# A full-height second product for the attention scores of a hybrid encoder kernel

## The chip, the core and the metric

The kernel runs on one NeuronCore of a Trainium2 chip (trn2). The metric is the device time of one execution in microseconds (us); lower is better. The core has a matrix engine (TensorE, written PE in the profile, with its weight loads as PEld), a vector engine (VectorE, DVE), a scalar engine (ScalarE, ACT) and a general engine (GpSimd, POOL). Each works through its own queue of instructions in order, and they wait for one another by semaphores. SyncE (SP) issues most transfers. Matrix products go to PSUM, which the kernel uses as 8 banks of 128x512 numbers.

## The reference

The model is a two-layer encoder on 512 positions of 1024 channels. Layer 0 has a differential softmax attention (4 heads, two maps per head, 64 channels per map) beside a recurrent branch; layer 1 has a Fourier mixer; each layer ends in a gated feed-forward net. The change touches the attention scores alone:

```python
s = jnp.einsum('bqhmd,bkhmd->bhmqk', qi, k) * scale      # 4 heads h, 2 maps m, d = 64
p = jax.nn.softmax(s - slopes * dist, axis=-1)
a = p[:, :, 0] - lam * p[:, :, 1]
o = jnp.einsum('bhqk,bkhd->bqhd', a, v)
o = rmsnorm(o, subln_g) * (1.0 - lam_init)
```

## The kernel before

Products run in a 32-bit format of the matrix engine that takes 12 significant bits of each number. A 32-bit number is therefore split into `hi` (rounded) and `lo` (the rest), and a product is made as hi·hi + hi·lo + lo·hi, three matmuls (`mm3`, lines 109 to 111). ACT makes `hi` by a copy, DVE makes `lo` by a subtraction (line 106 in `split`; for some weights POOL does it). Weights come in units of 1 MiB, as two halves `raw`, through three buffers, and are split into `whi` and `wlo`.

`proj_qk` (line 514) makes the queries and keys of two heads, channel by position: a PSUM tile `pqk` of 128 rows holds both maps of a head, 64 rows each (`halves`). For queries it builds, per map, a 128-row tile that stacks hi and lo of the map's 64 channels (lines 532 and 533): for map 0 it is [hi; lo], for map 1 [lo; hi]. For keys it builds per map [hi; hi] (two ACT copies, lines 539 and 540), and one tile `klo` for both maps with the key's rests (line 541, one DVE subtraction per map).

`scores(h, t)` makes the scores of head h and 128 queries t. Per map there are two products into one bank `psc`. The first (line 558) runs over all 128 rows: [hi; lo] against [hi; hi] gives hi·hi + lo·hi. The second (line 559) runs over the map's 64 rows alone: hi of the query against `klo`. Then DVE adds the position bias and finds the row maximum (line 561), negates it (line 563), ACT takes the exponential with its sum (through `act`, line 93), and DVE forms `p` from both maps (lines 566 to 568).

The loop over `steps` runs 16 steps (h, t). Step i issues `scores` of step i, a piece of other matrix work (`proj_qk(2)` in steps 0 to 7, `proj_yg` after that), two recurrent scans (lines 502 and 505, steps 0 to 3), and the later stages of earlier steps: `turn` of step i-2 transposes p into `paT` (line 580) and splits it into `aT`; `av` (tile `poT`) multiplies pairs of steps with the values; `norm_o` (lines 597 to 610, with the root on POOL at line 608) and `turn_o` (line 618) follow per head. After the loop the output projection starts (`proj_tok`, tile `pj`), with what is left of the last heads between its first products (`drain`).

Each engine's queue order is fixed when the kernel is built, by a scheduler that sees the program above and estimates times. A changed instruction can therefore move others on the same or other engines.

Of the kernel before, what the change touches and what calls it, by code (L numbers as in the profile page):

```python
# [16 lines left out]
P = 128  # L17
# [18 lines left out]
def encoder_kernel(  # L36
# [29 lines left out]
    def pair(name, dtype=F32):  # L66
        """two [128, 512] halves of a tile"""
        t_ = tile1k(name, dtype)
        return t_[:, 0:S], t_[:, S:2 * S]
# [7 lines left out]
    def f(ap):  # L77
        return ap.bitcast(F32)

    def order_after(ins, others):  # L80
        """ins stays behind others of its engine"""
        for b in others:
            tc.add_manual_dep(
                ins.ins, b.ins.name,
                mybir.DependencyInfo(mybir.DependencyClass.NoSync, mybir.DependencyReason.DATA),
                reason="order",
            )

    # Activations that need a table set run set by set, in program order.
# [10 lines left out]
    def split(hi, lo, src, hi_eng=A, lo_eng=V):  # L100
        """src = hi + lo exactly, both of 12 significant bits."""
        if hi_eng is A:
            A.copy(hi, src)  # L103
        else:
            hi_eng.tensor_copy(hi, src)
        lo_eng.tensor_tensor(out=lo, in0=src, in1=f(hi), op=ALU.subtract)  # L106
# [105 lines left out]
    def inv_rms(ssa, ssb, n):  # L212
        """((ssa + ssb) / n + eps) ** -0.5 of two [P, 1] sums, of which ssa comes first."""
        m0, m = sm("m"), sm("m")
        V.tensor_scalar(out=m0, in0=ssa, scalar1=n * EPS, scalar2=None, op0=ALU.add)
        V.tensor_scalar(out=m, in0=ssb, scalar1=m0, scalar2=1.0 / n, op0=ALU.add, op1=ALU.mult)  # L216
        return inv_sqrt(m)
# [18 lines left out]
    def pre_norm(t, g):  # L236
        """x tile t, normalised, as two halves"""
        xs_ = pair("xn")
        r = pre_stats(t, xs_)
        for h in range(2):  # L240
            sl = slice(h * S, (h + 1) * S)
            V.scalar_tensor_tensor(out=xs_[h], in0=xt[t][:, sl], scalar=r, in1=g[:, sl], op0=ALU.mult, op1=ALU.mult)
        xn[t] = xs_

    def turn_x(t):
        """the halves of pre_norm into hn as [channel, token], split"""
        for h, xh in enumerate(xn.pop(t)):
            pt = bank("pT")
            for k in range(4):
                T.transpose(pt[:, k * P:(k + 1) * P], xh[:, k * P:(k + 1) * P], ident)  # L250
            dst = slice(t * P, (t + 1) * P)
            pv = pt.rearrange("p (k c) -> p k c", c=P)
            split(hn["hi"][:, h * 4:h * 4 + 4, dst], hn["lo"][:, h * 4:h * 4 + 4, dst], pv)

    def post_norm(t, ps, g):
        """x tile t += rmsnorm(ps) * g"""
        ys = pair("y")
        ss = [sm("ss"), sm("ss")]
        for h in range(2):
            A.activation(ys[h], ps[h], AF.Square, accum_out=ss[h])  # L260
        r = inv_rms(ss[0], ss[1], D)
        for h in range(2):
            sl = slice(h * S, (h + 1) * S)
            y = ys[h]
            V.scalar_tensor_tensor(out=y, in0=ps[h], scalar=r, in1=g[:, sl], op0=ALU.mult, op1=ALU.mult)
            V.tensor_tensor(out=xt[t][:, sl], in0=xt[t][:, sl], in1=y, op=ALU.add)

    def proj_tok(ks, lhs, chunk, tail, finish, late=None, hook=None, spare=False):
        """[tok, D] = sum over the row tiles ks; the last `tail` of them token tile by
        token tile to the end, the others in chunks. With `spare`, two banks stay free  # L270
        and the last row tile is not needed until the first token tile ends."""
# [41 lines left out]
    def col_tiles(unit_list, consume, halves):  # L313
        """[col, tok] products of column tiles: unit_list holds (unit, column offset)."""
# [50 lines left out]
    # per-channel vectors: rows of 128, turned into columns by one transpose  # L365
# [56 lines left out]
    # lambda of the differential attention, on every partition  # L422
# [8 lines left out]
    # -(e1 - e2 + lam_init)  # L431
# [5 lines left out]
    # C * log_sigmoid(lam) = -C * (max(-lam, 0) + log1p(exp(-|lam|)))  # L437
# [24 lines left out]
    def make_gates(c):  # L462
        for d in range(2):
            g2 = pair("gate")
            for n, b_ in enumerate((ba, bi)):
                ps = bank("pg")
                o = (d * 4 + c) * P
                mm3(ps, [w[:, o:o + P] for w in ulru[n]], xcs[c], True, True)
                act(g2[n], ps, AF.Sigmoid, "sigmoid", bias=b_[:, d * 4 + c:d * 4 + c + 1])
            # i * xc  # L470
            last_ix[0] = G.tensor_tensor(out=g2[1], in0=g2[1], in1=xc[c], op=ALU.mult)
            gates[d, c] = g2

    # decays: a = exp(cl r) = 1 + q, q = expm1(cl r); sqrt(1 - a^2) = sqrt(-q (2 + q))
# [39 lines left out]
    def proj_qk(h0):  # L514
        """q and k of heads h0 and h0 + 1, in eight parts"""
        qh = {}
        for z in range(2):
            u = next_unit(1)
            for h in (h0, h0 + 1):
# [9 lines left out]
                if z == 0:  # L529
                    # [hi; lo] and [lo; hi]  # L530
# [4 lines left out]
                else:  # L535
                    # [hi; hi] twice, and lo
                    lo = tile1k("klo", F32R)[:, 0:S]
                    for m, sl in enumerate(halves):
                        A.copy(a[m][sl, :], ps[sl, :])
                        A.copy(a[m][halves[1 - m], :], ps[sl, :])  # L540
                        V.tensor_tensor(out=lo[sl, :], in0=ps[sl, :], in1=f(a[m][sl, :]), op=ALU.subtract)
# [6 lines left out]
    def scores(h, t):  # L548
        """p0 - lam (s0 / s1) p1 of unnormalised p; the norm that follows takes care of s0"""
# [5 lines left out]
        for m in range(2):  # L555
            sl = halves[m]
            ps = bank("psc")
            T.matmul(ps, lhsT=q_[m][:, t * P:(t + 1) * P], rhs=k_[m], start=True, stop=False)  # L558
            T.matmul(ps, lhsT=q_[m][sl, t * P:(t + 1) * P], rhs=klo[sl, :], start=False, stop=True)  # L559
# [13 lines left out]
    def turn(h, t):  # L573
        """[query, key] tile into [key, query], split"""
# [19 lines left out]
    def norm_o(h):  # L594
# [7 lines left out]
        # mean + eps s0^2  # L602
# [23 lines left out]
    def proj_yg():  # L626
        """gate columns, in eight parts"""
# [42 lines left out]
    def finish_step(i):  # L670
        """later stages of steps before i"""
# [27 lines left out]
    # what is left goes between the first products of the output projection  # L699
# [19 lines left out]
    def ffn(l, after, tail, hook=None):  # L719
# [11 lines left out]
        for u in range(NF // 2):  # L731
            # the first pair's products cover the norm's end: splits for later ones come after it
# [62 lines left out]
    # [p, (kt, cos|sin, c')]  # L795
# [10 lines left out]
    # over the positions: the last token tile after the others  # L806
# [17 lines left out]
    # over the channels of a group: E (even in k) and O (odd in k), F = E - O  # L824
# [16 lines left out]
    def mirror(c):  # L841
        """y[512 - k] = E + O, then y[k] = E - O in place of E"""
# [38 lines left out]
def _parts(a):  # L881
    """float64 -> [2, ...] float32: a value of 12 significant bits, and 12 bits of the rest."""
# [49 lines left out]
```

## Time and profile before

| | |
|---|---|
| time, median of 3 runs | 1058.29 us (1057.21 to 1058.57) |
| span of the profiled execution, first to last instruction | 1056.6 us |
| first products of the scores, line 558 | 32, median 494 ns each |
| second products of the scores, line 559 | 32, median 497 ns each |
| key rests, line 541 | 8 on DVE, median 690 ns each |
| the score products run from | 96.7 us to 186.5 us of the span |

The page gives the span of the profiled execution and not its whole time; the median of the runs is 1.7 us above the span, and that difference is taken as what lies around it. Rows of the timeline give the start, the duration, the engine, the source line, the operation with output<-inputs, its size, and in brackets the idle time of the engine just before it with what ended it. Durations of matmuls overlap, so the distance from one start to the next tells what a matmul costs, and the duration does not.

### The profile page before, as it was taken

How to read it: one execution, taken by the hardware profiler on the slowest of the kernel's cores; microseconds unless marked ns; L12 is line 12 of the kernel's file. 1: busy time of each engine (PE TensorE's matmuls, PEld its weight loads, DVE VectorE, ACT ScalarE, POOL GpSimd, SP SyncE). 2: the span in 40 equal slices, each digit the busy share in tenths (PEclk: the TensorE clock that was granted, in tenths of full speed). 3: DMA queues.
4: the chain of work that ended last, by engine and by line, in shares of the span. 5: the costliest groups of instructions: out<-in, count | busy, mean ns of one | idle time of the engine just before them, and what ended most of it. 6: DMA issues, size and time to landing. Idle time of an engine off the chain costs nothing.

```text
span 1056.6 us, 12277 instructions
## 1 busy us (share of the span) xinstructions
PE 1032.2 (98%) x4913; PEld 857.7 (81%) x4913; DVE 480.4 (45%) x760; ACT 391.1 (37%) x644; POOL 100.3 (9%) x94
## 2 busy tenths in 40 slices
PE   5999999999999999999999999999999999999997
PEld 4897677779888888888888888898888888888885
DVE  5969976754532332223233556645322223234304
ACT  5386676733522221122232455334221122223201
POOL 1057523211000000000100110100000000000000
PEclk9998999999999999999999999999999999999999
DMA  6531212311752333222533024027343223224002
GB/s 222 161 107 70 95 46 95 119 41 41 205 153 80 113 108 98 80 81 89 168 111 110 1 65 155 1 80 219 92 127 101 79 80 107 93 80 138 3 1 80
DMA packets 73123, 102.92 MB, mean 97 GB/s; under 512 B 3893, under 2 KB 61290, under 8 KB 73066
## 3 DMA queue, kind: packets, MB, share of 16 engines
q1 hardware_dynamic: 70442, 94.02, 28.7%
q0 software_dynamic: 2624, 8.13, 2.4%
q8 instruction: 38, 0.62, 0.2%
q14 instruction: 19, 0.16, 0.0%
HBM read 100.04 MB, written 2.10 MB: 97 GB/s over the span
## 4 chain that ended last, share of the span: by engine, by line
PE 94%; DVE 3%; ACT 1%; DMA 1%; issue 1%; POOL 0%; SPq 0%; DVEq 0%; POOLq 0%; ACTq 0%
PE pc L110 15%; PE pc L109 15%; PE pc L111 15%; PE pj L111 10%; PE pj L109 10%; PE pj L110 10%; PE pqk L109 1%; PE psc L559 1%; PE pqk L110 1%; PE pqk L111 1%; PE psc L558 1%; DMA raw<-in_w_in_dram 1%; PE pT L250 1%; PE pyg L109 1%; PE pv L111 1%; PE put L109 1%
## 5 line engine op out<-in xcount | busy, mean ns | idle before, releaser
L106 DVE TENSOR_TENSOR wlo<-raw,whi 128x1024 fp32r<-128x1024 f32 x158 | 190.9, 1232 | 272.2 <-ACT whi L103 221.1
L110 PE MATMUL pc<-hnlo,whi 128*128 128x512 f32 (+1 forms) x768 | 285.1, 372 | 0.0
L109 PE MATMUL pc<-hnhi,whi 128*128 128x512 f32 (+1 forms) x768 | 284.6, 372 | 0.5 <-ACT hnhi L103 0.5
L111 PE MATMUL pc<-hnhi,wlo 128*128 128x512 f32 (+1 forms) x768 | 284.9, 371 | 0.0
L103 ACT CAST whi<-raw 128x1024 fp32r<-128x1024 f32 x164 | 167.4, 1049 | 125.2 <-PE pj L110 31.0
L109 PEld LDWEIGHTS pc<-hnhi,whi 128*128 128x128 f32 x768 | 144.2, 188 | 26.1 <-ACT hnhi L103 1.0
L111 PEld LDWEIGHTS pc<-hnhi,wlo 128*128 128x128 f32 x768 | 144.7, 188 | 25.1
L110 PEld LDWEIGHTS pc<-hnlo,whi 128*128 128x128 f32 x768 | 144.7, 188 | 25.0 <-DVE hnlo L106 0.4
L109 PE MATMUL pj<-whi,gs 128*128 128x512 f32 x352 | 136.9, 389 | 0.0
L110 PE MATMUL pj<-wlo,gs 128*128 128x512 f32 x352 | 136.9, 389 | 0.0
L111 PE MATMUL pj<-whi,gs 128*128 128x512 f32 x352 | 136.9, 389 | 0.0
L93 ACT ACTIVATE gated<-pc 128x512 f32<-128x512 f32 x44 | 26.2, 597 | 268.6 <-PE pc L111 268.6
L729 DVE TENSOR_TENSOR gated<-gated,pc 128x512 f32<-128x512 f32 x44 | 30.2, 686 | 111.4 <-PE pc L111 111.4
L111 PEld LDWEIGHTS pj<-whi,gs 128*128 128x128 f32 x352 | 66.1, 188 | 13.8
L110 PEld LDWEIGHTS pj<-wlo,gs 128*128 128x128 f32 x352 | 66.1, 188 | 13.8
L109 PEld LDWEIGHTS pj<-whi,gs 128*128 128x128 f32 x352 | 66.1, 188 | 13.6
L209 POOL TENSOR_TENSOR r<-m,mhalf 128x1 f32<-128x1 f32 x32 | 17.5, 547 | 552.2 <-DVE m L216 552.2
L260 ACT ACTIVATE y<-pj 128x512 f32<-128x512 f32 x32 | 19.1, 597 | 82.3 <-PE pj L111 82.3
L103 ACT CAST gs<-gated 128x512 fp32r<-128x512 f32 x44 | 25.3, 618 | 52.2 <-PE pj L110 32.2
L106 DVE TENSOR_TENSOR gs<-gated,gs 128x512 fp32r<-128x512 f32 x44 | 28.4, 685 | 31.3 <-ACT gs L103 31.3
L106 POOL TENSOR_TENSOR wlo<-raw,whi 128x1024 fp32r<-128x1024 f32 x12 | 29.7, 2484 | 47.9 <-ACT whi L103 46.8
L93 ACT ACTIVATE p<-p,mx 128x512 f32<-128x512 f32 x32 | 23.1, 723 | 17.6 <-DVE mx L563 17.5
(190 smaller groups left out, 1282.5 us busy)
## 6 DMA issues: line engine op xcount, KB each, us to landing
raw<-in_w_ffn_gate_dram SPq DMA_DIRECT2D x44, 512.0 KB, 4.1
raw<-in_w_ffn_up_dram SPq DMA_DIRECT2D x44, 512.0 KB, 5.1
raw<-in_w_ffn_down_dram SPq DMA_DIRECT2D x44, 512.0 KB, 3.8
raw<-in_w_in_dram SPq DMA_DIRECT2D x20, 512.0 KB, 3.7
raw<-in_w_mix_out_dram SPq DMA_DIRECT2D x8, 512.0 KB, 3.3
raw<-in_w_fourier_out_dram SPq DMA_DIRECT2D x8, 512.0 KB, 4.3
pos<-in_dft_pos_dram POOLq DMA_DIRECT2D x8, 256.0 KB, 5.7
out_dram<-x SPq DMA_DIRECT2D x8, 256.0 KB, 2.1
```

Of the source, the lines that this page charges most:

```text
L93: ins = A.activation(out_, in_, func, **kw)
L103: A.copy(hi, src)
L106: lo_eng.tensor_tensor(out=lo, in0=src, in1=f(hi), op=ALU.subtract)
L109: T.matmul(ps, lhsT=l[0], rhs=r[0], start=start, stop=False)
L110: T.matmul(ps, lhsT=l[0], rhs=r[1], start=False, stop=False)
L111: T.matmul(ps, lhsT=l[1], rhs=r[0], start=False, stop=stop)
L209: G.tensor_tensor(out=r, in0=m, in1=mhalf[:, 0:1], op=ALU.pow)
L250: T.transpose(pt[:, k * P:(k + 1) * P], xh[:, k * P:(k + 1) * P], ident)
L260: A.activation(ys[h], ps[h], AF.Square, accum_out=ss[h])
L558: T.matmul(ps, lhsT=q_[m][:, t * P:(t + 1) * P], rhs=k_[m], start=True, stop=False)
L559: T.matmul(ps, lhsT=q_[m][sl, t * P:(t + 1) * P], rhs=klo[sl, :], start=False, stop=True)
L729: V.tensor_tensor(out=gated[fc], in0=gated[fc], in1=ps, op=ALU.mult)
```

## The change

The key rests are now built for each map as a 128-row tile [lo; lo] in place of 64 rows, so that the second product takes the whole stacked query: [hi; lo] against [lo; lo]. It adds the lo·lo part, which was left out before, and the number of matmuls stays. DVE makes each rest twice, once per half of the rows: 16 subtractions of 64x512 where there were 8. The tile pool serves the same number of tiles of the same size. (Comments were taken out as well; from the second added line on, lines up to 556 are numbered one higher.)

```diff
                 else:
-                    lo = tile1k("klo", F32R)[:, 0:S]
+                    lo = pair("klo", F32R)
                     for m, sl in enumerate(halves):
                         A.copy(a[m][sl, :], ps[sl, :])
                         A.copy(a[m][halves[1 - m], :], ps[sl, :])
-                        V.tensor_tensor(out=lo[sl, :], in0=ps[sl, :], in1=f(a[m][sl, :]), op=ALU.subtract)
+                        for to in halves:
+                            V.tensor_tensor(out=lo[m][to, :], in0=ps[sl, :], in1=f(a[m][sl, :]), op=ALU.subtract)
                     qks[h] = (qh[h], a, lo)
...
         for m in range(2):
-            sl = halves[m]
             ps = bank("psc")
             T.matmul(ps, lhsT=q_[m][:, t * P:(t + 1) * P], rhs=k_[m], start=True, stop=False)
-            T.matmul(ps, lhsT=q_[m][sl, t * P:(t + 1) * P], rhs=klo[sl, :], start=False, stop=True)
+            T.matmul(ps, lhsT=q_[m][:, t * P:(t + 1) * P], rhs=klo[m], start=False, stop=True)
```

The scheduler moves instructions of DVE, ACT, POOL and, in a few places, PE between the first scores and the output projection; the queue of SP is as it was. Three places follow.

On DVE, ahead of the first scores (`klo` is the key rest, `gate` the recurrent scans, `psc` the scores of step 0), before:

```order
L541 TENSOR_TENSOR klo_941<-pqk_915,qk_940 64x512
L505 SCALAR_TENSOR_TENSOR gate_563<-gate_563 128x512
L502 SCALAR_TENSOR_TENSOR gate_607<-gate_607 128x512
L541 TENSOR_TENSOR klo_941<-pqk_915,qk_940 64x512
L505 SCALAR_TENSOR_TENSOR gate_619<-gate_619 128x512
L502 SCALAR_TENSOR_TENSOR gate_695<-gate_695 128x512
L505 SCALAR_TENSOR_TENSOR gate_707<-gate_707 128x512
L502 SCALAR_TENSOR_TENSOR gate_719<-gate_719 128x512
L541 TENSOR_TENSOR klo_974<-pqk_948,qk_973 64x512
L561 ISA p_997,mx_1002<-psc_999,bias_839 128x512
```

and the same place with the change:

```order
L542 TENSOR_TENSOR klo_941<-pqk_915,qk_940 64x512 x2
L505 SCALAR_TENSOR_TENSOR gate_563<-gate_563 128x512
L502 SCALAR_TENSOR_TENSOR gate_607<-gate_607 128x512
L542 TENSOR_TENSOR klo_941<-pqk_915,qk_940 64x512 x2
L505 SCALAR_TENSOR_TENSOR gate_619<-gate_619 128x512
L502 SCALAR_TENSOR_TENSOR gate_695<-gate_695 128x512
L542 TENSOR_TENSOR klo_976<-pqk_950,qk_975 64x512 x2
L561 ISA p_1001,mx_1006<-psc_1003,bias_839 128x512
```

Each rest stands there twice, and one pair of scans has moved from ahead of the first line 561 to behind it (it stands ahead of the first line 566 in both).

On ACT, at the norm of head 0 (line 610 scales head 0's output, `p_1410` is step 8; the two rows of line 93 are the exponentials of its two maps), before:

```order
L93 ACTIVATE p_1410,sums_1411<-p_1410,mx_1415 128x512
L103 CAST whi_1432<-raw_1430 128x1024
L103 CAST whi_1438<-raw_1436 128x1024
L93 ACTIVATE p_1410,sums_1411<-p_1410,mx_1422 128x512
L610 ACTIVATE oT_1335<-po_1392,r_234_1404 128x128 x4
L103 CAST aT_1469<-paT_1471 128x4x128
```

and with the change (step 8 is `p_1418` here):

```order
L103 CAST whi_1440<-raw_1438 128x1024
L103 CAST whi_1446<-raw_1444 128x1024
L93 ACTIVATE p_1418,sums_1419<-p_1418,mx_1423 128x512
L610 ACTIVATE oT_1341<-po_1400,r_234_1412 128x128 x4
L93 ACTIVATE p_1418,sums_1419<-p_1418,mx_1430 128x512
L103 CAST aT_1477<-paT_1479 128x4x128
```

The scaling of head 0 now stands between the two exponentials.

On POOL, around the root of head 1's norm (line 608; `wlo` are weight rests), before:

```order
L106 TENSOR_TENSOR wlo_1439<-raw_1436,whi_1438 128x1024
L106 TENSOR_TENSOR wlo_1660<-raw_1657,whi_1659 128x1024
L608 TENSOR_TENSOR r_284_1631<-m_282_1625,mhalf 128x4
L106 TENSOR_TENSOR wlo_1666<-raw_1663,whi_1665 128x1024
L106 TENSOR_TENSOR wlo_1708<-raw_1705,whi_1707 128x1024
```

and with the change:

```order
L106 TENSOR_TENSOR wlo_1447<-raw_1444,whi_1446 128x1024
L106 TENSOR_TENSOR wlo_1668<-raw_1665,whi_1667 128x1024
L106 TENSOR_TENSOR wlo_1674<-raw_1671,whi_1673 128x1024
L608 TENSOR_TENSOR r_284_1639<-m_282_1633,mhalf 128x4
L106 TENSOR_TENSOR wlo_1716<-raw_1713,whi_1715 128x1024
```

The root now stands behind both weight rests of its unit.

## The prediction

> **What bounds the kernel now.** I begin with the first part of the page, the busy time of the engines, and the fourth, the chain that ended last:
>
> ```profile
> PE 1032.2 (98%) x4913; PEld 857.7 (81%) x4913; DVE 480.4 (45%) x760; ACT 391.1 (37%) x644; POOL 100.3 (9%) x94
> PE 94%; DVE 3%; ACT 1%; DMA 1%; issue 1%; POOL 0%; SPq 0%; DVEq 0%; POOLq 0%; ACTq 0%
> ```
>
> Over the whole span the matrix engine is the bound. But the change works between 95 and 200 us only, so the view by stages comes next (length, then busy us of PE, PEld, DVE, ACT, POOL, then the granted clock):
>
> ```profile
> 95.00:105.00 10.00, 7.73 (x23) 5.30 (x22) 9.91 (x8) 3.37 (x5) 9.99 (x5) 0.75 0.12 41
> 105.00:115.00 10.00, 10.00 (x34) 6.43 (x34) 9.68 (x17) 5.60 (x9) 7.14 (x4) 0.91 0.17 52
> 185.00:195.00 10.00, 10.00 (x54) 7.80 (x53) 6.97 (x17) 9.10 (x16) 4.76 (x2) 1.00 0.26 78
> 195.00:205.00 10.00, 8.59 (x51) 7.09 (x50) 7.72 (x13) 7.49 (x15) 1.38 (x1) 1.00 0.45 133
> ```
>
> PE has no idle time from 105 us to the loop's end, but DVE is 70 to 99% busy, ACT up to 91%, and just after the loop PE does wait. For whom, the list of waits says (total us, times, longest), for PE, DVE and ACT in this stretch:
>
> ```profile
> PE psc L559 <- DVE klo L541: 2.3, 1, 2.3
> PE pj L109 <- ACT oT L610: 1.4, 1, 1.4
> DVE c L566 <- ACT p L93: 14.1, 14, 2.9
> ACT p L93 <- DVE mx L563: 17.5, 17, 2.3
> ACT qk L539 <- PE pqk L111: 2.4, 1, 2.4
> ACT aT L103 <- PE paT L580: 1.5, 2, 0.8
> ACT oT L592 <- PE poT L111: 1.4, 1, 1.4
> ```
>
> This is the view on which I rest most. DVE and ACT wait for one another 31 times (31.6 us). For PE, DVE never waits between 112 and 196 us, and ACT waits four times, 5.3 us in all. So beside PE runs a second chain, DVE to ACT and back, that is about as long as PE's and hardly held up by PE. The timeline shows where they meet, at the output projection's first products:
>
> ```profile
> 191.09 0.16 DVE L566 RECIPROCAL c<-sums 128x1 f32<-128x1 f32 x1 [1.53 <-ACT p L93]
> 195.90 0.17 DVE L606 TENSOR_SCALAR m<-m 128x4 f32<-128x4 f32 x1
> 196.15 1.38 POOL L608 TENSOR_TENSOR r<-m,mhalf 128x4 f32<-128x4 f32 x1 [3.56 <-DVE m L606]
> 197.56 1.14 ACT L610 ACTIVATE oT<-po,r 128x128 f32<-128x128 f32 x4 [1.71 <-POOL r L608]
> 198.76 0.50 PE L109 MATMUL pj<-whi,mx 128*128 128x512 f32 x1 [1.41 <-ACT oT L610]
> ```
>
> The norm of head 2 goes DVE, POOL, ACT, and PE waits 1.41 us for it. What comes behind 198.76 us starts when this chain is done.
>
> **What the change takes from PE.** One step of the loop, at full clock:
>
> ```profile
> 120.45 0.60 PE L580 MATMUL paT<-ident,p 128*128 128x128 f32 x4
> 120.80 0.48 PE L558 MATMUL psc<-qk,qk 128*128 128x512 f32 x1
> 121.21 0.50 PE L559 MATMUL psc<-klo,qk 64*128 64x512 f32 x1
> 121.64 0.50 PE L558 MATMUL psc<-qk,qk 128*128 128x512 f32 x1
> 122.07 0.50 PE L559 MATMUL psc<-klo,qk 64*128 64x512 f32 x1
> 122.50 0.50 PE L109 MATMUL pqk<-hnhi,whi 128*128 128x512 f32 x1
> 122.84 0.40 PE L110 MATMUL pqk<-hnlo,whi 128*128 128x512 f32 x1
> 123.08 0.40 PE L111 MATMUL pqk<-hnhi,wlo 128*128 128x512 f32 x1
> 123.32 0.40 PE L109 MATMUL pqk<-hnhi,whi 128*128 128x512 f32 x1
> ```
>
> From start to start, a 128-row product behind a 128-row product takes 0.24 us; into and out of a 64-row product it takes 0.41 to 0.43. The five starts from 120.80 to 122.84 take 2.04 us. With 128 rows throughout, five would take 5 x 0.24 = 1.20, and up to 0.1 more behind the transposes, so a step loses 0.74 to 0.84 us; I take 0.8. Fourteen of the 16 steps run at full clock: 14 x 0.8 = 11.2 us that PE alone could win.
>
> [...]
>
> **What it adds on DVE.** Eight more subtractions. These rows give their price, and the place of the first:
>
> ```profile
> 86.67 1.28 DVE L533 TENSOR_TENSOR qk<-pqk,qk 64x512 fp32r<-64x512 f32 x2
> 95.34 0.68 DVE L541 TENSOR_TENSOR klo<-pqk,qk 64x512 fp32r<-64x512 f32 x1
> 99.66 0.69 DVE L541 TENSOR_TENSOR klo<-pqk,qk 64x512 fp32r<-64x512 f32 x1
> 100.41 0.79 PE L559 MATMUL psc<-klo,qk 64*128 64x512 f32 x1 [2.27 <-DVE klo L541]
> ```
>
> L533 has the same shape and also writes the other half of the rows; two in a row take 1.28, so one more costs about 0.6. Two of the new ones lie ahead of 100.41: PE's wait there grows from 2.27 to about 3.5 us. Queued behind it are the second half of head 2's first query product and step 1. PE's balance is then -11.2 + 1.3 = -9.9 us, were PE alone to decide.
>
> For the second chain I go through the terms, each with its bounds.
>
> - **Four rests of heads 0 and 1: +2.4.** DVE is busy for 9.91 and 9.68 us of the first two stages above, so 4 x 0.6 fall on the chain in full; the moved pair of scans stays ahead of the first L566.
> - **Four rests of heads 2 and 3: +1.2** (0 to +2.4). DVE has gaps there; half is the middle.
> - **ACT's waits for PE: -3.7** (-5.3 to 0). These go if PE is early. The longest is
>
> ```profile
> 143.23 0.58 ACT L539 CAST qk<-pqk 64x512 fp32r<-64x512 f32 x1 [2.43 <-PE pqk L111]
> 144.43 0.68 DVE L541 TENSOR_TENSOR klo<-pqk,qk 64x512 fp32r<-64x512 f32 x1 [0.86 <-ACT qk L540]
> 146.46 0.16 DVE L566 RECIPROCAL c<-sums 128x1 f32<-128x1 f32 x1 [0.73 <-ACT p L93]
> 185.03 0.59 ACT L592 COPY oT<-poT 128x512 f32<-128x512 f32 x1 [1.36 <-PE poT L111]
> ```
>
>   and of its 2.43 us DVE felt 0.86 + 0.73 = 1.6. With the 1.36 at 185.03, and about 0.7 of the two waits of L103, that is 3.7.
> - **Head 0's norm: +1.1** (0 to +1.1). The four L610 (1.14 us in the row at 197.56) now stand ahead of the exponential that step 8's L566 waits for.
> - **Head 1's norm: 0** (-1.1 to +2.4). Its root on POOL now stands behind a second weight rest, 2.38 us in the row below; in return its L610 stands behind both exponentials of step 12, which saves up to 1.1. The weight rests release buffers for SP's transfers in the same order as before.
>
> ```profile
> 149.98 2.38 POOL L106 TENSOR_TENSOR wlo<-raw,whi 128x1024 fp32r<-128x1024 f32 x1 [18.81 <-ACT whi L103]
> ```
>
> - **The rest of the new order: 0** (-1.2 to 0). In two steps an `aT` rest of 0.6 us moves into a wait for the exponential.
>
> Sum: 2.4 + 1.2 - 3.7 + 1.1 = **+1.0 us**, with ends at 2.4 - 1.1 - 1.2 - 5.3 = -5.2 and 2.4 + 2.4 + 1.1 + 2.4 = +8.3. PE's gain does not enter, since PE, once ahead, waits for p, for `aT` and for the norms. What hides the gain is the chain's length, and if it were shorter than I think, the gain would come through. Against the profiled execution: span 1056.6 + 1.0 = 1057.6, and with the 1.7 us between the span and the median of the runs, 1059.3.
>
> **The rivals.**
>
> *PE's gain comes through: 1058.3 - 9.9 = 1048.4.* For it speaks the first part of the page and the chain that ended last, which runs through PE for 94%. Against it: the tail already waits for the second chain, and what that chain waits for is almost never PE. It needs the chain to lose about 10 us, while its lower end is -5.2.
>
> *The chain shortens by its lower end: 1058.3 - 5.2 = 1053.1.* For it: DVE sits idle for 14.1 us behind exponentials, into which the new subtractions and the new order may fit.
>
> *PE loses its clock while it waits: 1061.5.* PE that is 0.8 us a step faster than what feeds it must wait somewhere. If it does so at one place, these rows say what follows (columns as above, PE only, then the clock):
>
> ```profile
> 98.00:99.00 1.00, 0.14 (x1) 1.00 0.00 0
> 100.00:101.00 1.00, 0.59 (x1) 0.50 0.00 0
> 106.00:107.00 1.00, 1.00 (x4) 0.58 0.00 0
> 107.00:108.00 1.00, 1.00 (x4) 1.00 0.00 0
> ```
>
> After the 2.27 us gap the granted clock was 0.5 for some 6.5 us; after the 1.41 us gap at 198.76 it stayed at 1.00 (the row 195 to 205). So from a wait between 1.4 and 2.3 us on, PE works 6.5 us at half clock and loses 3.2. Where the chain's lead over PE is smaller than that, as at the output projection, most of it shows: +1.0 + 2.2 = +3.2. For it: PE's 9.9 us must go somewhere. Against it: spread over 14 steps they are 0.7 us each, too short.
>
> [...]
>
> *The slower turn is not due to the row count, so nothing leaves PE: 1062.4.* Then ACT's waits stay too: +1.0 + 3.7 = +4.7, less 0.6 of it in gaps. Against it: every 64-row product shows it, and no other of 512 columns behind one of its kind.
>
> **How the numbers follow.** A measurement of this kernel tells about 0.2%, 2.1 us, from no change. The chain as summed, within 2.1 us of no change: 0.41, and the forecast is its time, 1059.3. PE's gain in full: 0.16. The lower end of the chain: 0.13. The clock: 0.25, and with it the chain's upper half. Nothing leaves PE: 0.05. So faster 0.29, same 0.41, slower 0.30. The range from 1048 to 1064 takes in the first rival and, on the other side, the last with some of the chain's upper end (+8.3 would be 1066.6). The likeliest case alone would have 1056.2 to 1060.4.
>
> **What would show it.** L559 as 128x128 with starts 0.24 apart shows the first term right. PE idle in the loop and before the output projection's first products, some 8 to 11 us more than before, ended by DVE or ACT, shows that the second chain holds; the row of L608 for head 2 within 2 us of 196.15 puts a number on it. A PE without gaps up to 176 us and an L608 near 187 would prove the first rival; clock digits below 9 after 110 us the third. The forecast is wrong at its root if DVE's waits for ACT's exponentials shrink from 14.1 us to well under 8.

## The result, and the profile after

| | before | after |
|---|---|---|
| runs, us | 1057.21 to 1059.18 | 1062.51, 1062.53, 1064.93, 1065.07 |
| median, us | 1058.43 | 1063.73 |
| ratio to before, 95% interval | | 1.0053 [1.0039, 1.0067] |
| span of the profiled execution, us | 1056.6 | 1060.7 |

The change makes the kernel 0.5% slower; the forecast was no change, 1059.3. The same views follow as for the kernel before, in the same order. The first and fourth parts of the page:

```profile
PE 1026.3 (97%) x4913; PEld 860.9 (81%) x4913; DVE 488.3 (46%) x768; ACT 390.7 (37%) x644; POOL 98.2 (9%) x94
PE 88%; DVE 6%; ACT 2%; issue 2%; POOL 1%; DMA 1%; SPq 0%; POOLq 0%; DVEq 0%; ACTq 0%
```

PE is busy 5.9 us less and has lost 6 points of the chain that ended last, 3 to DVE and 1 each to ACT, POOL and issue. The timeline of PE shows that the products themselves became cheaper, as forecast: 0.23 us from start to start, with no slower turn.

```profile
110.60 0.39 PE L558 MATMUL psc<-qk,qk 128*128 128x512 f32 x1
110.83 0.39 PE L559 MATMUL psc<-klo,qk 128*128 128x512 f32 x1
111.06 0.39 PE L558 MATMUL psc<-qk,qk 128*128 128x512 f32 x1
111.28 0.39 PE L559 MATMUL psc<-klo,qk 128*128 128x512 f32 x1
```

Where that time went is in the list of waits from 95 to 200 us (total us, times, longest) and in the stages (length, busy us of PE, PEld, DVE, ACT, POOL, granted clock):

```profile
PE psc L559 <- DVE klo L542: 3.9, 1, 3.9
PE paT L580 <- DVE p L568: 2.8, 1, 2.8
PE poT L109 <- ACT aT L103: 2.8, 2, 2.0
PE poT L110 <- DVE aT L106: 2.0, 2, 1.0
DVE c L566 <- ACT p L93: 10.4, 10, 2.9
```

```profile
105.00:115.00 10.00, 9.39 (x39) 7.38 (x37) 9.81 (x16) 5.50 (x9) 6.30 (x5) 0.94 0.17 52
185.00:195.00 10.00, 8.03 (x47) 6.69 (x46) 7.46 (x19) 7.44 (x15) 4.97 (x3) 1.00 0.33 111
195.00:205.00 10.00, 9.02 (x39) 7.39 (x38) 8.52 (x15) 7.81 (x15) 1.81 (x2) 0.66 0.62 186
```

PE's four rows come to 11.5 us (13.6 with its smaller ones), where it waited 3.7 us before, and it works part of the stage from 195 us at half clock (0.66 on the mean, 1.00 before). The end of the second chain came later, not earlier. L606 is the scaling of head 2's sums, L592 the copy of head 3's product:

```profile
198.74 0.17 DVE L606 TENSOR_SCALAR m<-m 128x4 f32<-128x4 f32 x1
198.99 1.38 POOL L608 TENSOR_TENSOR r<-m,mhalf 128x4 f32<-128x4 f32 x1 [3.56 <-DVE m L606]
207.88 0.59 ACT L592 COPY oT<-poT 128x512 f32<-128x512 f32 x1 [2.10 <-PE poT L111]
```

L606 stood at 195.90 before: **+2.8 us** in the loop. L592 stood here before:

```profile
203.75 0.59 ACT L592 COPY oT<-poT 128x512 f32<-128x512 f32 x1 [0.79 <-PE poT L111]
```

From L606 to it took 7.85 us and takes 9.14 now, **+1.3 us** more. Nothing differs behind that (2.8 + 1.3 = 4.1 = 1060.7 - 1056.6).

Two places in the loop stand out. (A step is measured from one L566 to the next: step n ends with the L566 of step n, so the first step runs from step 0's L566 to step 1's.) The first step took 5.04 us before:

```profile
112.64 0.16 DVE L566 RECIPROCAL c<-sums 128x1 f32<-128x1 f32 x1 [0.15 <-ACT p L93]
112.84 0.26 DVE L567 SCALAR_TENSOR_TENSOR c<-c,nlam,sums 128x1 f32<-128x1 f32 x1
113.13 0.75 DVE L568 SCALAR_TENSOR_TENSOR p<-p,c 128x512 f32<-128x512 f32 x1
117.68 0.17 DVE L566 RECIPROCAL c<-sums 128x1 f32<-128x1 f32 x1
```

It takes 8.09 us with the change:

```profile
112.87 0.14 DVE L566 RECIPROCAL c<-sums 128x1 f32<-128x1 f32 x1
113.03 1.29 POOL L506 TENSOR_TENSOR gate<-gate,gate 128x512 f32<-128x512 f32 x1 [2.54 <-DVE c L566]
113.04 1.29 DVE L567 SCALAR_TENSOR_TENSOR c<-c,nlam,sums 128x1 f32<-128x1 f32 x1
114.28 2.34 POOL L106 TENSOR_TENSOR wlo<-raw,whi 128x1024 fp32r<-128x1024 f32 x1
114.37 2.79 DVE L568 SCALAR_TENSOR_TENSOR p<-p,c 128x512 f32<-128x512 f32 x1
120.96 0.17 DVE L566 RECIPROCAL c<-sums 128x1 f32<-128x1 f32 x1
```

L567 and L568 took 0.26 and 0.75 us before, and now run beside GpSimd's sum (L506) and weight rest (L106): L567 ends at 114.33 us and the sum at 114.32, L568 at 117.16 and the rest at 116.62. That is 1.03 + 2.04 = 3.07 us more, the whole difference of the step. L561, which reads the bank `psc`, took its usual 0.69 us at 113.91 us in the kernel before, beside the same weight rest (113.62 to 116.14 us). The second place is step 8:

```profile
150.47 1.40 DVE L542 TENSOR_TENSOR klo<-pqk,qk 64x512 fp32r<-64x512 f32 x2
151.90 1.43 DVE L604 SCALAR_TENSOR_TENSOR s<-sums 128x4 f32<-128x4 f32 x1
154.98 0.73 ACT L93 ACTIVATE p<-p,mx 128x512 f32<-128x512 f32 x1 [3.19 <-DVE mx L563]
157.85 0.17 DVE L566 RECIPROCAL c<-sums 128x1 f32<-128x1 f32 x1 [2.91 <-ACT p L93]
```

Both maps' scores of step 8 now stand behind two rests and a stalled L604 (1.43 us beside GpSimd's weight rest of 150.93 to 153.31 us; 0.15 us alone, at 197.35 us), ACT waits 3.19 us for them, and DVE then 2.91 us for ACT, with head 0's four L610 between the exponentials. Step 8 took 6.86 us and takes 9.53. The stall of L604 is not new, it was longer before; but then only the second of the two maps' scores stood behind it:

```profile
150.11 2.26 DVE L604 SCALAR_TENSOR_TENSOR s<-sums 128x4 f32<-128x4 f32 x1
153.32 0.16 DVE L566 RECIPROCAL c<-sums 128x1 f32<-128x1 f32 x1 [0.55 <-ACT p L93]
```

### The profile page after: what moved, and what is told of

Same layout as the page of the kernel before. It is cut to its first block, busy times and chain, and to the rows that moved or that the text cites. A ratio compares the mean times of both kernels' runs of the same rounds, so it can differ in the third digit from the quotient of the medians.

```text
span 1060.7 us, 12280 instructions
## 1 busy us (share of the span) xinstructions
PE 1026.3 (97%) x4913; PEld 860.9 (81%) x4913; DVE 488.3 (46%) x768; ACT 390.7 (37%) x644; POOL 98.2 (9%) x94
## 4 chain that ended last, share of the span: by engine, by line
PE 88%; DVE 6%; ACT 2%; issue 2%; POOL 1%; DMA 1%; SPq 0%; POOLq 0%; DVEq 0%; ACTq 0%
PE pc L110 15%; PE pc L109 15%; PE pc L111 15%; PE pj L111 10%; PE pj L110 10%; PE pj L109 10%; DVE klo L542 1%; DMA raw<-in_w_in_dram 1%; PE pT L250 1%; DVE p L568 1%; DVE p L561 1%; PE pv L111 1%; PE put L109 1%; PE put L110 1%; PE pxr L110 1%
## 5 line engine op out<-in xcount | busy, mean ns | idle before, releaser
L106 DVE TENSOR_TENSOR wlo<-raw,whi 128x1024 fp32r<-128x1024 f32 x158 | 191.2, 1233 | 272.9 <-ACT whi L103 221.4
L106 DVE TENSOR_TENSOR gs<-gated,gs 128x512 fp32r<-128x512 f32 x44 | 28.5, 686 | 31.3 <-ACT gs L103 31.3
L106 POOL TENSOR_TENSOR wlo<-raw,whi 128x1024 fp32r<-128x1024 f32 x12 | 29.0, 2432 | 49.5 <-ACT whi L103 49.5
```

## The experiments

The theory at the start (T1): the second chain sets the time, and what costs is the eight subtractions, their collisions and new order, and the clock that PE loses in its longer waits. The rivals: only the subtractions; only PE's clock; the 128-row product itself. All twelve runs are below. The fourth column is the time from the first `klo` on DVE to L606 of head 2 (the line number shifts by a few), which leaves out that the loop starts up to 1.8 us earlier or later from one execution to the next; the last is the time from there to the copy of head 3's product.

| run | median, us | ratio to before | first klo to L606, us | L606 to copy, us |
|---|---|---|---|---|
| before | 1058.43 | | 95.34 to 195.90: 100.56 | 7.85 |
| after | 1063.73 | 1.0053 [1.0039, 1.0067] | 95.26 to 198.74: 103.48 | 9.14 |
| e1_cross | 1056.10 | 0.9977 [0.9968, 0.9986] | 95.70 to 194.73: 99.03 | 7.86 |
| e2_doubled | 1065.43 | 1.0061 [1.0048, 1.0073] | 94.87 to 200.97: 106.10 | 7.84 |
| e3_late | 1062.36 | 1.0041 [1.0028, 1.0053] | 96.37 to 198.50: 102.13 | 9.20 |
| e4_warm | 1064.51 | 1.0057 [1.0043, 1.0071] | 96.44 to 202.76: 106.32 | 9.61 |
| e5_twice01 | 1058.20 | 0.9999 [0.9990, 1.0008] | 95.54 to 195.42: 99.88 | 7.86 |
| e6_twice23 | 1060.64 | 1.0024 [1.0014, 1.0033] | 95.30 to 198.74: 103.44 | 9.44 |
| e7_norest | 1061.75 | 1.0029 [1.0018, 1.0039] | 94.67 to 196.10: 101.43 | 9.17 |
| e8_last64 | 1063.30 | 1.0040 [1.0027, 1.0053] | 95.06 to 198.56: 103.50 | 7.85 |
| e9_again | 1063.26 | 1.0048 [1.0035, 1.0060] | 94.64 to 200.77: 106.13 | 8.48 |
| e10_fill | 1062.31 | 1.0042 [1.0029, 1.0055] | 94.68 to 198.15: 103.47 | 9.51 |
| e11_cross2 | 1055.76 | 0.9974 [0.9963, 0.9985] | 95.85 to 193.27: 97.42 | 7.86 |
| e12_fill2 | 1062.24 | 1.0042 [1.0028, 1.0056] | 94.91 to 198.34: 103.43 | 8.49 |

### The wide product without the subtractions (e1_cross)

```diff
-            sl = halves[m]
...
-            T.matmul(ps, lhsT=q_[m][sl, t * P:(t + 1) * P], rhs=klo[sl, :], start=False, stop=True)
+            T.matmul(ps, lhsT=q_[m][:, t * P:(t + 1) * P], rhs=klo, start=False, stop=True)
```

> The kernel before, with one change: the second product runs over 128 rows against the one tile of rests it already has, [lo of map 0; lo of map 1], so no subtraction is added and the order on VectorE, ScalarE and GpSimd stays that of before. It adds to each map's scores a product of the two maps' rests, which the reference does not have. Theory T1 (the chain of VectorE, ScalarE and GpSimd sets the time; what the change costs is its eight subtractions, their place and the clock that TensorE loses in its waits): faster than the kernel after by at least 3 us, within -3 and +1 of the kernel before, so 1055.5 to 1059.5; TensorE is ahead by some 8 us and waits for VectorE or ScalarE at three to five places. Rival A (TensorE decides, and only the wait for the rests kept its gain away): about 1047 to 1049. Rival B (the 128-row products with the halved clock behind their waits are the loss): as the kernel after, 1062 to 1064.

1056.10, in the span of T1. PE's gain of about 11 us does not come through (Rival A, 1047 to 1049), and the wide product is no loss (Rival B): alone it makes the kernel some 2.5 us faster. With DVE's order unchanged PE waits 0.4 us or more at ten places; T1 had three to five.

### The subtractions without the wide product (e2_doubled)

```diff
-            T.matmul(ps, lhsT=q_[m][:, t * P:(t + 1) * P], rhs=klo[m], start=False, stop=True)
+            sl = halves[m]
+            T.matmul(ps, lhsT=q_[m][sl, t * P:(t + 1) * P], rhs=klo[m][sl, :], start=False, stop=True)
```

> The kernel after with its eight extra subtractions and their tiles, but the second product over 64 rows as before: the loss by VectorE alone. Theory T1: the rests cost the chain the same as in the kernel after, some 2 to 3 us; ScalarE keeps its waits for TensorE (up to 3.7 us, of which part lies in gaps), and the 1.3 us of halved clock at the output projection go: 1060 to 1063, slower than the kernel before. Rival B (the product's shape and the clock are the loss): 1058 to 1059, no difference from the kernel before. Rival C (the 128-row products do win on balance, the subtractions lose more): 1064 or above.

1065.43: above T1's number and in Rival C's. T1 had the subtractions too cheap. They cost 106.10 - 100.56 = 5.5 us in the loop, more than the whole change loses there (2.9), and the wide product takes 2.6 of it back. The granted clock is 1.00 at the output projection here (from 106.4 to 208.8 us throughout), and there the time is that of before, 7.84 us.

### The last scan held back (e3_late)

```diff
-            V.tensor_tensor_scan(out=u, data0=a_, data1=u, initial=0.0, op0=ALU.mult, op1=ALU.add)
+            s_ins = V.tensor_tensor_scan(out=u, data0=a_, data1=u, initial=0.0, op0=ALU.mult, op1=ALU.add)
...
+            if c == 3:
+                order_after(s_ins, [p_ins[0, 0]])
...
-        V.scalar_tensor_tensor(out=pr[0], in0=pr[1], scalar=c1, in1=pr[0], op0=ALU.mult, op1=ALU.add)
+        p_ins[h, t] = V.scalar_tensor_tensor(out=pr[0], in0=pr[1], scalar=c1, in1=pr[0], op0=ALU.mult, op1=ALU.add)
```

> The kernel after, with the last forward scan and the pair behind it held back until the first step's p on VectorE, so that GpSimd's sum and weight rest do not start while that step's L567 and L568 run. Theory T1 with collisions (L567 and L568 of the first step took 1.29 and 2.79 us beside GpSimd's work, 0.26 and 0.75 before, and the chain loses these 3.1 us): L567 and L568 back to about 0.3 and 0.7, L606 of head 2 earlier by 1.5 to 3 us, 1060.5 to 1062.3. If the stalls cost nothing, since the time behind them is gained back in waits for the exponentials: 1063.4 to 1064. If the work only collides with the next step: the same.

1062.36, just above T1's span, and the gain that there is did not come in T1's way: GpSimd's weight rest came 2.1 us earlier against the step and met L567 (2.12 us) in place of L568 (0.75 us), and the scan of 1.22 us stood behind. The first step took 8.02 us again; of the 1.35 us gained up to L606, 1.1 lie ahead of it (first klo to its L566: 17.61 us after, 16.47 here). The edit moves a collision, and does not remove it.

### Without the weight rest of that moment (e7_norest)

```diff
...
-        split(hi, lo, raw, hi_eng=V if i in HI_DVE else A, lo_eng=G if i in LO_POOL else V)
+        if (i, h) == (8, 1):
+            A.copy(hi, raw)
+            lo = hi
+        else:
+            split(hi, lo, raw, hi_eng=V if i in HI_DVE else A, lo_eng=G if i in LO_POOL else V)
```

> The kernel after without one weight rest: the second half of the unit of key columns of heads 2 and 3 (the one that GpSimd works on at 114.28 us in the kernel after) has its whi used in the place of its wlo, so those products are not the reference's. Theory T1 with collisions: L567 and L568 of the first step lose only what GpSimd's sum costs them (up to 1.1 us) and not the 2.0 us of the weight rest, so the first step takes 5.1 to 6.2 us in place of 8.09, and L606 of head 2 comes 1.9 to 3 us earlier: 1060.5 to 1062. If the stall is not GpSimd's doing: first step 8.1 us, 1063 to 1064. If the time is gained back later: first step short, L606 of head 2 within 0.7 us of the kernel after.

The timeline of DVE in this kernel, first step:

```profile
112.43 1.29 DVE L572 SCALAR_TENSOR_TENSOR c<-c,nlam,sums 128x1 f32<-128x1 f32 x1
114.37 0.75 DVE L573 SCALAR_TENSOR_TENSOR p<-p,c 128x512 f32<-128x512 f32 x1
117.99 0.16 DVE L571 RECIPROCAL c<-sums 128x1 f32<-128x1 f32 x1
```

The sum's 1.29 us stays, L568's counterpart is back at 0.75, the step takes 5.73 us, and 103.48 - 101.43 = 2.05 us reach L606 (the fifth step is 0.4 us longer). So L568's stall is GpSimd's doing, and most of it counts; 1061.75 is in T1's span.

### One pair of heads at a time (e5_twice01, e6_twice23)

```diff
-                    lo = pair("klo", F32R)
+                    lo = pair("klo", F32R) if h0 == 0 else [tile1k("klo", F32R)[:, 0:S]] * 2
...
-                        for to in halves:
+                        for to in (halves if h0 == 0 else (sl,)):
```

and `h0 == 2` in the other.

> The kernel after, with the doubled rests for heads 0 and 1 only; heads 2 and 3 share one tile of rests between the maps as in e1_cross (which adds products of the two maps' rests for these heads). VectorE's order is that of the kernel after up to the rests of heads 2 and 3, that of before behind. Theory T1: the four early rests cost some 0.3 us up to the first step's reciprocal and 3.0 us in the first step, where GpSimd's weight rest meets L567 and L568; the rest of the loop runs as in e1_cross: from the first klo to L606 of head 2 102.2 to 102.7 us, 1059 to 1061. If the early rests are hidden and the late ones are what costs: 99 to 100 us and 1056 to 1057.5.

> The reverse: the doubled rests for heads 2 and 3 only, heads 0 and 1 share one tile of rests as in e1_cross. VectorE's order is that of before up to the rests of heads 2 and 3, that of the kernel after behind. Theory T1: the first step takes 5.04 us again, the rest as in the kernel after, 100.1 to 100.7 us from the first klo to L606 of head 2, and the output projection loses up to 1.3 us at half clock: 1057.5 to 1060. If the late rests are what costs: 102 to 103 us and 1061 to 1064.

Both fell outside T1's numbers, the first below (99.88), the second above (103.44). They are nearer to the other reading that both expectations name, that the late rests are what costs: 99.88 lies in its 99 to 100, 103.44 above its 102 to 103. Against e1_cross, 99.03, the early rests would cost 0.9 us and the late ones 4.4, the two together 5.3, and the kernel after shows 4.45. What made the parts not add up is, by the profiles that follow below, the clock. e1_cross had half clock from 138.3 to 141.7 us, just ahead of a long seventh step; e6_twice23 had it from 137.5 to 140.9 and from 158.0 to 161.4 us, behind waits of about 1 us, and its steps 7 and 10 took 5.39 and 5.19 us where the kernel after took 3.84 and 3.87. e5_twice01 had none there. My rule of the prediction, that a single wait above 1.4 to 2.3 us halves the clock, does not give this.

### Head 3 with narrow products (e8_last64)

```diff
-            T.matmul(ps, lhsT=q_[m][:, t * P:(t + 1) * P], rhs=klo[m], start=False, stop=True)
+            sl = halves[m] if h == 3 else slice(0, P)
+            T.matmul(ps, lhsT=q_[m][sl, t * P:(t + 1) * P], rhs=klo[m][sl, :], start=False, stop=True)
```

> The kernel after, with the second product of head 3 alone over 64 rows again; every instruction stands in the same place on every engine. TensorE is then some 3 us later at the output projection and does not wait 1.97 us at 194.00. Theory T1 with the clock: the granted clock stays at 1.00 from 194 to 202 us and the time from L606 of head 2 to the copy of head 3's product falls from 9.14 to 7.85 us (7.84 in e2_doubled), so 1.3 us less than the kernel after unless ScalarE's waits for TensorE come back: 1061.5 to 1063. If the clock there costs nothing: 9.1 us again and no gain.

Its timeline at the output projection (L607 and L593 are L606 and L592 of the kernel after):

```profile
198.56 0.17 DVE L607 TENSOR_SCALAR m<-m 128x4 f32<-128x4 f32 x1
206.41 0.59 ACT L593 COPY oT<-poT 128x512 f32<-128x512 f32 x1 [0.81 <-PE poT L111]
```

7.85 us, as before, with L606 as late as in the kernel after (103.50 and 103.48 us). The granted clock was 1.00 from 120.3 to 209.1 us. So the 1.3 us at the output projection are the clock's. The whole table bears this out: the six profiles without half clock behind 190 us take 7.84 to 7.86 us there, the two with one stretch of 3.4 us at half clock (e9_again, e12_fill2) 8.48 and 8.49, the five with two (6.8 us) 9.14 to 9.51. (In e4_warm, with 9.61, eight added products stand in the way.) PE comes there too early with the wide products and the new queue order together: in e1_cross, e5_twice01 and e11_cross2, with wide products and the order of before behind the loop, the clock holds, and so it does in e2_doubled, with the new order and narrow products. The profiled execution took 1059.4 against 1060.7 us; the median, 1063.30, does not show it beside the spread of the runs.

### Dummy products in the wait (e4_warm)

```diff
+    def warm(h):
+        poT[h] = bank("poT")
+        for i in range(8):
+            T.matmul(poT[h], lhsT=vs[i % 4][0][:, 0:P], rhs=vs[(i + 1) % 4][0], start=True, stop=True)
...
-        0: lambda: (av(last, 0), turn(last, NT - 2)),
+        0: lambda: (warm(last), av(last, 0), turn(last, NT - 2)),
```

> The kernel after, with eight more 128x512 products into the bank that the next real product overwrites, put where TensorE waits 1.97 us at 194.00 in the kernel after. Theory T1 (of the 4.1 us lost at the output projection 1.3 come from the halved clock behind that wait): the clock stays at 1.00 from 194 to 202 us, L592 of head 3 comes about 1.3 us earlier against L610 of head 2 than in the kernel after, 1062 to 1062.8. If the clock there costs nothing: 1063.4 to 1064. If the extra products themselves are in the way (8 x 0.24 us, or 8 x 0.43 at half clock): 1064 to 1066.

Inconclusive. Eight products changed the scheduler's order behind the loop; PE then waited 2.5 us for an `aT` and the clock halved at 201 us instead. It also had half clock from 160.3 to 167.1 us, and a step 10 of 6.69 us, although its order up to there is that of the kernel after.

### The clock's grid (e9_again, e11_cross2)

In each trace, all changes of the granted clock turned out to lie on one grid of 3.41 us. (In the kernel after, half clock lasts 3.42 us from 102.77, 6.82 us from 116.43 and 6.83 us from 194.93 us, with 10.24 and 71.68 us at whole clock between: 1, 2, 2, 3 and 21 stretches, 71.68 / 21 = 3.41.) So I made a second theory (T2) of it, and ran two kernels unchanged for a second profile.

> The kernel after, unchanged, for a second profile. Theory T2: the granted clock is set anew at the marks of a grid of 3.41 us that runs on its own; a stretch between two marks in which TensorE was busy for less than about half is followed by one at half clock, so the same waits cost a run time or not, depending on where they lie to the grid. Then the runs spread over 2 us or more as before; if the profile has half clock between 157 and 167 us, step 10 takes 5.2 to 6.7 us where it took 3.87, and 1.3 to 2.9 us more go; if not, step 10 takes 3.8 to 3.9. All changes of the clock lie on one grid of 3.41 us. Rival (the clock follows the length of one wait, and a wait as long as the 1.97 and 2.83 us of the first profile always halves it, one of 0.86 us never): the half clock stands at the same places as in the first profile.

> The kernel of e1_cross, unchanged, for a second profile. Its first one had half clock from 138.3 to 141.7 us and a seventh step of 6.76 us (6.10 before). Theory T2: where the clock stays whole from 134 to 144 us, the seventh step takes 4.5 to 5.2 us, and from the first klo to L606 of head 2 it is 97.0 to 97.8 us in place of 99.03; where it halves again, 98.7 to 99.3. If the half clock was not what made the seventh step long: 6.7 us at either clock. Median 1055 to 1057.

The windows of the kernel after, cut at its grid (length, PE's busy us, clock):

```profile
157.39:160.80 3.41, 2.03 (x9) 1.00 0.44 143
160.80:164.21 3.41, 3.41 (x21) 1.00 0.05 16
191.52:194.93 3.41, 1.44 (x10) 1.00 0.25 66
194.93:198.35 3.42, 2.44 (x10) 0.50 0.62 209
198.35:201.76 3.41, 3.41 (x14) 0.50 0.61 180
201.76:205.17 3.41, 3.41 (x19) 1.00 0.59 161
```

and of the same kernel in e9_again:

```profile
154.67:158.08 3.41, 2.11 (x11) 1.00 0.21 82
158.08:161.49 3.41, 2.96 (x7) 0.50 0.48 154
161.49:164.91 3.42, 3.42 (x10) 0.50 0.02 5
164.91:168.32 3.41, 3.41 (x24) 1.00 0.01 2
```

Each stretch has one clock from mark to mark. The grid lies elsewhere in the second execution (its mark at 117.12 us is 22.48 us behind the first `klo`, the mark at 116.43 us of the first execution 21.17), and the same wait (0.86 us in both) falls differently into it: one execution keeps its clock, the other works 6.8 us at half clock. The busy shares do not say which: 2.03 of 3.41 us kept the clock and 2.11 lost it, so both, 0.60 and 0.62, lie in a band in which either happened (0.46 to 0.62 over the 14 traces), and what decides there is not shown. (1.44 of 3.41 at the output projection lies below the band.) Step 10 took 6.52 us in place of 3.87, and 106.13 - 103.48 = 2.65 us is just that. Over all profiles with the doubled late rests and wide products, step 10 is long only where half clock stands beside it: 5.19 to 6.69 us in e6_twice23, e4_warm and e9_again, 3.80 to 3.87 us in the six others. In e11_cross2 and e1_cross it is the other way; the windows around 138 us and the row of ACT that waits for PE, first e1_cross, then e11_cross2:

```profile
134.87:138.28 3.41, 1.69 (x13) 1.00 0.00 0
138.28:141.70 3.42, 3.42 (x13) 0.50 0.00 0
```

```profile
144.29 0.58 ACT L539 CAST qk<-pqk 64x512 fp32r<-64x512 f32 x1 [3.09 <-PE pqk L111]
```

```profile
135.50:138.91 3.41, 2.74 (x20) 1.00 0.00 0
138.91:142.32 3.41, 3.41 (x17) 1.00 0.00 0
```

```profile
142.81 0.58 ACT L539 CAST qk<-pqk 64x512 fp32r<-64x512 f32 x1 [1.48 <-PE pqk L111]
```

With the clock whole, ACT waits 1.6 us less, the seventh step takes 5.15 in place of 6.76 us, and 97.42 in place of 99.03 us are needed up to L606. Both of T2's forecasts held in these two profiles. With 97.42, the execution without that loss, as the base, the early rests cost 99.88 - 97.42 = 2.5 us and the late ones, on top of them, 103.48 - 99.88 = 3.6. Late rests alone are e6_twice23's 103.44 less the 1.55 and 1.32 us by which its steps 7 and 10 were longer than in the kernel after: 100.6, or 3.1 above the base. So the parts do add up, to about half a us, once the clock is taken out; that these two steps were long by the clock is inferred from e9_again and e11_cross2, not shown for e6_twice23 itself.

The steps tell where the late rests' 3.6 us come from, for both e5_twice01 and the kernel after work at whole clock from 123.3 to 194.9 us. Steps 6 to 8 lose 2.9, steps 9 to 11 win back 1.5, steps 12 to 14 lose 1.6, and 0.5 come behind them. Steps 12 to 14 hold head 1's norm. Its four L610 moved out of step 12 (8.54 us in e5_twice01, 7.79 in the kernel after) into step 13 (5.33 and 6.32), and its L621 moved from step 13 into step 14 (3.25 and 4.61), where the scores' L563 stands behind it and ACT waits; first e5_twice01, then two rows of the kernel after:

```profile
181.24 0.75 DVE L621 SCALAR_TENSOR_TENSOR mx<-pmT,subg,mx 128x512 fp32r<-128x512 f32 x1
```

```profile
185.64 0.74 DVE L621 SCALAR_TENSOR_TENSOR mx<-pmT,subg,mx 128x512 fp32r<-128x512 f32 x1
187.20 0.72 ACT L93 ACTIVATE p<-p,mx 128x512 f32<-128x512 f32 x1 [2.49 <-DVE mx L563]
```

This is read from the rows; no run moves that norm alone.

### Products that hold the clock (e10_fill, e12_fill2)

```diff
+        if (h, j) == (1, 1):
+            for i in range(6):
+                T.matmul(poT[h][:, 256:512], lhsT=vs[i % 4][0][:, 0:P], rhs=vs[(i + 1) % 4][0][:, 0:256], start=True, stop=True)
```

is e12_fill2; e10_fill had five of 512 columns ahead of head 2's first product.

> The kernel after, with five more 128x512 products of values into the bank that head 2's first product then overwrites, put just ahead of that product, where TensorE waits 0.86 and 0.52 us around 159 us; all other instructions keep their order. Theory T2: no half clock between 157 and 167 us in any run, step 10 at 3.8 to 3.9 us, and the slow ones of the runs (about 1065) go: median 1061.5 to 1063, at least 0.5 us below that of the unchanged kernel in the same job. If the spread has another cause: the same median and spread as the unchanged kernel. If the products are in the way: step 9 or 10 longer by up to 1.2 us.

> The extra products of e10_fill stood 20 us behind the wait that they were meant for (that wait is at the second product of head 1, not the first of head 2). Here six products of 256 columns stand where TensorE waits 0.86 us at 158.84 in the kernel after, in the half of head 1's bank that its next product overwrites; all other instructions keep their order. Theory T2: TensorE's busy share of the stretch around 159 us rises from 0.60 to about 0.8, no half clock between 154 and 168 us, step 10 at 3.8 to 3.9 us, every run below 1064, median 1061.8 to 1062.8. If the spread of the unchanged kernel (1061.9 to 1065.3) has another cause: the same spread, with runs above 1064. If the products are in the way: step 10 longer by up to 0.5 us in all runs.

e10_fill's products stood 20 us behind their place, so that its median, 1062.31, lies in T2's span does not come from filling that wait. In e12_fill2 they fill it; the timeline of PE:

```profile
157.47 0.87 PE L590 MATMUL poT<-v,v 128*128 128x256 f32 x6
158.51 0.38 PE L109 MATMUL poT<-aT,v 128*128 128x256 f32 x1 [0.17 <-ACT aT L103]
```

No half clock there, step 10 at 3.80 us, five runs from 1061.44 to 1063.05, where nine of the unchanged kernel lay between 1061.88 and 1065.31. That is as T2 has it, but two things speak for caution. The five runs of e10_fill, which leaves the wait at 159 us as it was, lie as close together (1062.27 to 1063.40). And the mean granted clock does not tell the long runs from the short ones: the kernel after has 0.989 and 0.990 at 1062.51 and 1062.53 us, and 0.989 at 1064.93 and 1065.07. The intervals of e12_fill2 and e9_again overlap as well. So that the grid makes the spread of the runs is possible, and not shown.

## Why the prediction was wrong

- **What the change takes from PE: right.** 0.23 us from start to start, and PE's waits in the list grew from 3.7 to 13.6 us (all of PE's rows), 9.9 more, within the 8 to 11 that the prediction named: the gain is spent in waiting. (That it is the very 9.9 of the prediction's sum is chance, since PE also worked more time at half clock.)
- **That the second chain sets the time: right.** DVE's waits for exponentials went from 14.1 to 10.4 us, not well under 8, and without the subtractions PE's gain still does not come through (e1_cross). The first rival, 1048.4, falls, and with the second chain growing by 2.9 us so does that of its lower end. That growth is beyond the prediction's own sign: L608 for head 2 came at 198.99, 2.8 us behind 196.15 and not within 2.
- **ACT's waits for PE, -3.7: nearly.** The wide product alone brought 100.56 - 97.42 = 3.1 us, and beside the doubled rests 2.6.
- **Four rests of heads 0 and 1, +2.4: right in size by luck, wrong in place.** 2.5 by e5_twice01. Ahead of the first L566 they cost 0.3 us, since the scans there collide less with GpSimd's work (seven scans took 13.4 us before and 10.9 after; one took 1.23 us alone, at 110.61 us after, and 2.60 us beside a weight rest, at 109.11 us before); then 3.07 us come from GpSimd's work that now falls on L567 and L568, and some 0.9 is won back in steps 6 and 7. The prediction had put GpSimd's collisions into no term.
- **Late rests and norms, +1.2 + 1.1 + 0 + 0: too low.** They cost 3.6 us. The rests and head 0's norm come to some 1.4 from step 6 to step 11, less than the 2.3 given to them; head 1's norm, put at 0, comes to 1.6 from step 12 to step 14. That lies within its bounds (-1.1 to +2.4), but the prediction saw only the two ends: it shortened step 12 as the lower bound has it, and what lengthened the next two steps was not the root on POOL but its L610 and L621 in their new places.
- **Two steps failed: terms of the chain that were sized too low, and a sum that held no term for the clock.** The chain grew by 2.9 us in place of 1.0: head 1's norm cost 1.6 where 0 stood, ACT's waits gave 0.6 less, the end of the loop cost 0.5, and the rests and head 0's norm some 0.9 less. That alone would be 1061.2. The clock I had as a rival of its own, 1061.5, with a chance of 0.25, in place of a cost that comes with the forecast: a PE 10 us ahead of its feeder must wait, and I had judged waits spread over 14 steps harmless. The sign that the prediction named for it, a clock below 9 behind 110 us, came at 116.4 and 194.9 us. It adds 1.3 us at the output projection in the first profile, and 2.65 at step 10 besides in executions like e9_again. The first profile's 4.1 us are so accounted for. The median is 1.2 us above this profiled execution; the second loss could be the reason, which no run shows.
- **The rule for the clock: wrong.** Not the length of one wait decides, and the 6.5 us at half clock that the prediction read off were two stretches of 3.41 us (100.01 to 106.84 us before). 0.86 us, with what else was idle in its stretch, halved the clock in e9_again and not in the first profile; 1.84 us at 120.6 us halved it in e11_cross2, and 1.82 us at the same place in e1_cross did not. What the traces show in its place, PE's busy share of a whole stretch, is counted in the last section.
- **The last rival,** that nothing leaves PE, falls with the first point.

The version that beats both kernels is e1_cross: 1056.10 and 1055.76 in two jobs, 0.2 to 0.3% below before. It adds to the scores a product of the rests of two different maps; the lo·lo part that the kernel before leaves out is a product of two rests as well, and how large either is was not measured.

## What to carry to other kernels

An engine that is made faster than what feeds it wins only what its waits cost others, and it pays for its own waits if its clock follows its activity, as here (1.3 us at the output projection): put that cost into the sum, not beside it. Before adding work to a feeder, look for a layout in which the existing tile already serves; here one tile of rests for both maps gave the wide product without a new subtraction. Where a profile is taken once, compare stretches between fixed events, since the start (by up to 1.8 us) and the clock's grid differed from one execution to the next here.

## What the hardware showed that I had not expected

In the 14 traces, from about 94 to 212 us, the granted clock changed only on a grid of 3.41 us, whose place differed from execution to execution. Cut at their grids, a stretch at whole clock was followed by one at half clock in 25 of 25 cases where PE's busy share was 0.45 or less, in 9 of 28 between 0.46 and 0.62, and in none of 349 above. A stretch at half clock was followed by another in 15 of 15 cases up to a share of 0.77, in 3 of 5 between 0.85 and 0.88, and in none of 32 above. What decides within the middle bands is open. Each stretch at half clock takes, by estimate, some 1.6 us of work from PE (its products of 512 columns start 0.43 us apart there and 0.23 us at whole clock: 3.41 x (1 - 0.23 / 0.43)). In the kernel after that showed in the time only where PE was not ahead: the 6.8 us from 116 to 123 us cost the kernel after nothing (steps 1 to 3 took 8.09, 3.31 and 3.70 us; with whole clock there, in e12_fill2, 8.12, 3.31 and 3.70).

Beside GpSimd's sums and weight rests, L567 and L568 took longer. L567, an operation on one column, took 0.21 to 0.26 us alone; beside GpSimd it took 0.88, 1.29 and 1.74 us in the kernel after and 1.31 us before, and ended each time within 0.02 us of GpSimd's work. L568 took 0.73 to 0.75 us alone and 2.58 and 2.79 us beside a weight rest in the kernel after; without that rest, in e7_norest, the 2.79 us were 0.75 again. No run leaves out a sum beside L567. L542 kept its 0.70 us beside the rest at 150.93 us, as L561 did before.
